# A pool of weight pieces moved to the top of the memory, and a ring of its own for each operand of the MLP's second product

## The chip, the cores and the metric

The kernel runs on one core of one Trainium2 chip. The metric is the device time of one execution in microseconds (us). Before the change the median of three runs is 2457.29 us (2456.69 to 2461.17).

## What is computed

The reference is one layer of a hybrid encoder on 1024 tokens of width 1024, all in float32:

```
shift1, scale1, gate1, shift2, scale2, gate2 = split(silu(c) @ w_ada + b_ada, 6)
h = rms_norm(x, norm1_w) * (1 + scale1) + shift1
q, k, v, xBC, z, dt, gates = split(h @ w_in)            # 1024, 256, 256, 3072, 2048, 64, 2048 columns
attn = attention(rope(rms_norm(q)), rope(rms_norm(k)), v)      # 16 heads on 4 key heads
ssd  = mamba2(silu(conv5(xBC)), z, dt)                  # forward and backward, chunks of 128
merged = sigmoid(gates[:1024]) * (attn @ w_attn_out) + sigmoid(gates[1024:]) * (ssd @ w_ssd_out)
x = x + gate1 * (merged @ w_o)
h2 = rms_norm(x, norm2_w) * (1 + scale2) + shift2
x = x + gate2 * (relu(h2 @ w_mlp1) ** 2 @ w_mlp2)       # 4096 hidden columns
```

## The kernel before, in words

**Split operands.** Each float32 operand is split into a high part, cast to fp32r by ScalarE (`A.copy`, line 173 of the profile), and the rest as a low part, subtracted by VectorE or GpSimd (line 159). A product is three matmuls per 128 rows of the contraction: high by high, high by low, low by high, most of them with 512 moving columns. A call is `matmul(out, stationary, moving)`. The profile writes a matmul as out<-moving,stationary, so `pp<-t4h,wop` moves the tile t4h past weights from wop.

**Memory.** A tile pool takes a stretch of every partition's memory; a tag in it is a ring of `bufs` slots, and tags lie in the order in which they are first asked for. Pools open from the bottom ("left") or from the top (`side="right"`), and close in the reverse order; a later pool that lies on the same stretch waits, tile by tile, for the last users. In the kernel before the 224 KB of a partition are laid out so (KB from the bottom): constants to 20, `act` (32 tiles of 2 KB for activations) 20 to 84, then by stage, left | right:

- start and projections to q, k, v, dt and z: `p0` (84 to 153), then `p1` (84 to 163), `p1m` (108 to 120) | `tw` 164 to 216 with, upward, traw (8), twh (20), twl (20), zst (4), and `scan` 216 to 224
- from line 768 on `wp`, 84 to 108: wraw, whi, wlo, two slots of 4 KB each, for pieces of weights
- convolution inputs and conv (lines 830 to 975): `st` 108 to 156 (u2, u3, u4), `p2` 156 to 210
- attention (985 to 1140): `p3k` 108 to 140 (k1, k2, v1, q1), `p3` 140 to 212 (zall, ost, nm, pf, ph at 153 to 177, pl at 177 to 201, and small ones)
- scan of the state space part, with the output products woven in (1145 to 1395): `p4` 108 to 212
- merge (1400 to 1490): `wop` 108 to 124, `p5` 124 to 158 | `mp` 160 to 224: 32 tiles of 2 KB, first g2 (32 tiles), then wo in the same slots
- w_o, norm and the MLP's first product (1495 to 1860): `wop`, `p6`, later `c1p` and `p7`, 108 to 159 | `hp` 160 to 224: tag ops, 24 tiles (T2, T3, T4, high and low, four each) at 160 to 208, and tmp at 208 to 224
- MLP's second product (1865 to 2000): `c1p` 108 to 118, `p8` 118 to 158: ac, gate2, held slots o3 (2 of 4 KB), more slots o2 (5 of 4 KB) | `hp`, whose ops slots now hold accumulators

In a ring of 2 KB tiles the first tile takes the lowest slot, the next the highest, and then downward: T2's first high tile lies at 160, the next tile at 206, and T4 lies at 162 to 176. g2 and wo take `mp` in the same way, the half-0 tiles (wo: columns 0 to 511) at 194 to 222 and the half-1 tiles at 162 to 192 downward.

**Moving operands.** In the projections to q, k, v and z (`gemm_tm`, lines 506 to 524; `first_mm`, 372 to 380) the weights move (twh, twl, twh) and the activations are stationary. In conv (`product`, 912 to 919), in `gemm_cm` (lines 195 to 216: gates, attention and state space output products) and in the MLP's first product (`product`, 1497 to 1506) weights from `wp` are stationary and activations move. In attention the scores move k1 and k2 (1036, 1038), the values move ph and pl (1090 to 1093), and 128-column transposes of pf (1053) stand between them, four at a time. In the merge g2 moves (1483 to 1485), in w_o the tiles woh and wol (1550 to 1552).

**The MLP's first product** is one level of Strassen: for each of 16 pairs of columns the products with T2, T1, T3, B22 and T4 follow each other, twelve matmuls each (T1 and B22 lie in `act`); B11 and B21 come before them in 9 pairs, in the others earlier.

**The MLP's second product** runs three rounds of seven Strassen products of four steps (84 steps, twelve matmuls of 512 columns each) and a last plain round. `prepare(n)` splits the stationary operand a and the moving operand b of step n, `LA` = 3 steps ahead (`LA0` = 2 steps are made while the first product still runs). Both take slots from one ring, a and b in turn: whi, wlo, whi, wlo, wraw, wraw, held, held, more x5. In the plain round a takes more slots; the b of its first four steps, two tiles a step, take the same first eight slots (`held`: whi, wlo, whi, wlo, wraw, wraw, held, held) and stay for both halves of the rows; its other b tiles lie in `act`.

**Order of the work.** The tile framework puts instructions in order by a plan made when the kernel is built; where `manual_schedule` names engines, their order is as written (TensorE in attention, scan and z of group 2; TensorE, VectorE, ScalarE and SyncE in the start). SyncE (SP) issues most DMAs, ScalarE some, each in its own order.

Of the kernel before, what the change touches and what calls it, by code (L numbers as in the profile page):

```python
# [91 lines left out]
def block(ctx: ExitStack, tc: tile.TileContext, ia, out, upto=99, dbg=None):  # L92
# [51 lines left out]
    s1 = cp.tile([P, 8], F32, name="s1")  # L144
    s2 = cp.tile([P, 8], F32, name="s2")
    scs = ExitStack()
    sp = scs.enter_context(tc.tile_pool(name="scan", bufs=1, side="right"))
# [69 lines left out]

    def mod_acc(pool, sl, bufs=3, mb=2):
        acc = pool.tile([P, D], F32, name="macc", tag="macc", bufs=mb)
        for k in range(KT):  # L220
            wt = pool.tile([P, D], F32, name="wada", tag="wada", bufs=bufs)
# [6 lines left out]
        return acc  # L228

# [11 lines left out]
    twp = tws.enter_context(tc.tile_pool(name="tw", bufs=1, side="right", reuse_waits="tile"))  # L241

    def tw_raw(srcs):

        raw = twp.tile([P, 2, 512], F32, name="traw", tag="traw", bufs=2)
        c0 = 0
        for src in srcs:
            w = src.shape[1]
            dma(raw[:, :, c0:c0 + w], src.rearrange("(k p) c -> p k c", p=P))
            c0 += w  # L250
        return raw

# [18 lines left out]
    with tc.tile_pool(name="p0", bufs=1) as p0, tc.tile_pool(name="ps0", bufs=1, space=PSUM) as ps0:  # L271
# [263 lines left out]

    def mod_stream(pool, psum, part):

        for sl, mi, gt in ((3, 2, None), (4, 3, None), (2, None, g_d[0]), (5, None, g_d[1]))[2 * part:2 * part + 2]:
            acc = yield from mod_acc(pool, sl, bufs=2, mb=1)
            if gt is None:  # L540
                mod_col(acc, sl, mi, psum())
            else:
                row = pool.tile([1, D], F32, name="grow", tag="wada", bufs=2)
                dma(row, b_ada[sl * D:(sl + 1) * D].unsqueeze(0))
                for hf in range(2):
                    ns = slice(hf * 512, (hf + 1) * 512)
                    ps = psum()
                    T.matmul(ps[0:1], ones[:, 0:1], acc[:, ns], start=True, stop=True)
                    tt(V, row[:, ns], ps[0:1], row[:, ns], ALU.add)
                dma(gt.unsqueeze(0), row)  # L550
            yield 1
        if part == 0:
            scale_col(s2, 3, N2)

    with tc.tile_pool(name="p1", bufs=1, reuse_waits="tile") as p1, \
# [112 lines left out]
        def dt_stream():  # L668
# [34 lines left out]
            for nm, m, h0 in (("ef", LE, 0), ("sf", GT, 0), ("cf", ones, 0), ("eb", GE, 32), ("sb", LT, 32), ("cb", ones, 32)):  # L703
                if nm in ("ef", "eb"):
# [94 lines left out]
    with tc.tile_pool(name="p1m", bufs=1, reuse_waits="tile") as p1m, tc.tile_pool(name="ps1m", bufs=1, space=PSUM) as ps1m:  # L799

        mods = mod_stream(p1m, lambda: ps1m.tile([P, 512], F32, name="psm", tag="psm", bufs=2), 1)
# [193 lines left out]
    with tc.tile_pool(name="p3k", bufs=1, reuse_waits="tile") as p3k, \  # L995
# [3 lines left out]
        def gates_stream(pool, psp, i0, i1, bufs=2, e_lo=None):  # L999
# [5 lines left out]
            yield from gemm_cm(psp, "psg", [w_cols(w_in, OFF_G + i * P) for i in range(i0, i1)], hhi, hlo, evac, bufs=bufs, e_lo=e_lo)  # L1005

        def attn_stream():

# [4 lines left out]
            def load_head(h):  # L1013
                g = h // 4
                if h % 4 == 0:
                    k1, k2, v1 = (p3k.tile(shp, F32R, name=nm, tag=nm, bufs=2)
                                  for nm, shp in (("k1", [P, S]), ("k2", [P, S]), ("v1", [P, NT, P])))
                    dma(k1.bitcast(F32), k1_d[g])
                    kv[g] = k1, k2, v1
                qs[h] = p3k.tile([P, S], F32R, name="q1", tag="q1", bufs=2)  # L1020
# [23 lines left out]
            def turn(u, hf):  # L1044
# [3 lines left out]
                if j == 0:  # L1048
                    phs[b, hf] = p3.tile([P, 4, 512], F32R, name="ph", tag="ph", bufs=3)
                    pls[b, hf] = p3.tile([P, 4, 512], F32R, name="pl", tag="pl", bufs=3)  # L1050
                pt = ps3.tile([P, 4, P], F32, name="pst", tag="pst", bufs=2)
# [624 lines left out]
    with tc.tile_pool(name="p7", bufs=1, reuse_waits="tile") as p7:  # L1676
# [91 lines left out]
        def operand(x, slot):  # L1768
            t = slot()
            split(t[:, 0], t[:, 1], x)  # L1770
            return t

        def prepare(n):
# [266 lines left out]
```

## Time and profile before

| | us |
|---|---|
| median of three runs | 2457.29 |
| profiled execution | 2455.24 |
| its span, first to last instruction | 2453.4 |
| TensorE busy (97% of the span), 11307 matmuls | 2387.5 |
| VectorE busy | 1706.5 |
| ScalarE busy | 1092.0 |
| GpSimd busy | 829.2 |

The profile lists busy time by engine, groups of instructions (line, engine, operation, tiles, count, busy time, mean of one, idle time before and who ended it), the chain of work that ended last, and a timeline. Matmuls are pipelined, and the duration of one (389 ns and more) overlaps the next; what a matmul costs is the distance from its start to the next start. PE is TensorE, PEld its weight loads, DVE is VectorE, ACT is ScalarE, POOL is GpSimd, SP is SyncE. The mean granted TensorE clock is 0.993.

### The profile page before, as it was taken

What the parts mean: (1) busy time and instruction counts of PE and PEld (TensorE: products, weight loads), DVE (VectorE), ACT (ScalarE), POOL (GpSimd) and SP (SyncE); (2) the same over time, 40 slices, a digit from 0 to 9 for tenths busy, and PEclk for the clock granted to TensorE, in tenths of its full rate; (3) what the DMA queues carried; (4) which work ended last, traced back from release to release, by engine and by line L of the source; (5) the groups of instructions that cost most, each with busy time, mean ns of one, the idle gap of its engine ahead of it and who ended that gap; (6) DMA issues with size and microseconds to landing.
All of it is one profiled execution on the core that took longest, in us unless ns stands there. A gap on an engine that the chain in (4) does not pass through costs nothing.

```text
span 2453.4 us, 32245 instructions
## 1 busy us (share of the span) xinstructions
PE 2387.5 (97%) x11307; PEld 1900.2 (77%) x11307; DVE 1706.5 (70%) x2325; ACT 1092.0 (45%) x1884; POOL 829.2 (34%) x637
## 2 busy tenths in 40 slices
PE   8999999999989999999989999999999999999999
PEld 4998877888867777777767767787787888788887
DVE  5876435777756666666577796558568887767794
ACT  5455413555566666666333343354242222364430
POOL 0221107666611111110356665534006885023200
PEclk9999999999999999999999999999999999999999
DMA  7664751333531212111667765486325554654422
GB/s 257 185 184 139 255 170 65 95 103 111 183 114 52 91 52 80 57 53 48 223 207 222 223 209 177 142 282 202 125 86 193 196 174 159 231 172 142 153 79 83
DMA packets 288596, 366.53 MB, mean 149 GB/s; under 512 B 33962, under 2 KB 168850, under 8 KB 288434
## 3 DMA queue, kind: packets, MB, share of 16 engines
q1 hardware_dynamic: 216246, 288.77, 36.9%
q10 hardware_dynamic: 72187, 75.70, 9.1%
q8 instruction: 90, 1.47, 0.2%
q14 instruction: 73, 0.59, 0.1%
HBM read 250.54 MB, written 113.84 MB: 149 GB/s over the span
## 4 chain that ended last, share of the span: by engine, by line
PE 84%; DVE 7%; DMA 3%; issue 2%; ACT 2%; POOL 0%; ACTq 0%; SPq 0%; DVEq 0%; POOLq 0%
PE pst L1053 5%; PE psg L211 4%; PE psg L213 4%; PE psg L212 4%; PE pp L1503 4%; PE pp L1505 4%; PE pp L1504 4%; PE p L1919 3%; PE p L1918 3%; PE p L1917 3%; PE psc L916 3%; PE psc L917 3%; PE psc L918 3%; PE psq L518 3%; PE psq L519 3%; PE psq L517 3%
## 5 line engine op out<-in xcount | busy, mean ns | idle before, releaser
L1040 DVE TENSOR_REDUCE nm<-pss 128x1 f32<-128x1024 f32 x128 | 156.7, 1225 | 125.2 <-PE pss L1038 122.8
L1042 ACT ACTIVATE pf<-pss,nm 128x1024 f32<-128x1024 f32 x128 | 142.8, 1116 | 98.9 <-PE pst L1053 96.3
L159 DVE TENSOR_TENSOR pl<-pst,ph 128x512 fp32r<-128x512 f32 x256 | 167.6, 683 | 27.1 <-ACT ph L173 27.0
L1053 PEld LDWEIGHTS pst<-masks,pf 128*128 128x128 f32 x1024 | 117.5, 140 | 73.3 <-issue 33.3
L517 PE MATMUL psq<-twh,hh 128*128 128x512 f32 (+1 forms) x448 | 168.3, 380 | 3.0 <-ACT twh L173 3.0
L518 PE MATMUL psq<-twl,hh 128*128 128x512 f32 (+1 forms) x448 | 169.3, 379 | 0.9 <-DVE twl L159 0.9
L173 ACT CAST ph<-pst 128x512 fp32r<-128x512 f32 x256 | 145.7, 585 | 54.9 <-PE pst L1053 38.2
L1053 PE MATMUL pst<-masks,pf 128*128 128x128 f32 x1024 | 157.3, 276 | 13.0 <-DVE pl L159 10.6
L519 PE MATMUL psq<-twh,hl 128*128 128x512 f32 (+1 forms) x448 | 168.6, 377 | 0.0
L159 POOL TENSOR_TENSOR av<-av,rz 64x512 f32<-64x512 f32 x32 | 41.9, 1310 | 348.1 <-issue 99.3
L1917 PE MATMUL p<-o,o 128*128 128x512 f32 x400 | 153.6, 390 | 3.0 <-ACT o L173 1.6
L1918 PE MATMUL p<-o,o 128*128 128x512 f32 x400 | 155.2, 389 | 0.2 <-DVE o L159 0.2
L1919 PE MATMUL p<-o,o 128*128 128x512 f32 x400 | 153.7, 389 | 0.0
L173 ACT CAST wop<-ws 128x512 fp32r<-128x512 f32 x116 | 71.8, 621 | 124.4 <-PE pp L1505 78.7
L862 DVE SCALAR_TENSOR_TENSOR tap<-pad,cwT,tap 128x1024 f32<-128x1024 f32 x96 | 123.4, 1285 | 5.2 <-ACT tap L860 3.8
L159 POOL TENSOR_TENSOR ws<-r,r 128x512 f32<-128x512 f32 x29 | 41.4, 1428 | 220.3 <-DMA r<-in_w_mlp_dram 168.9
L159 POOL TENSOR_TENSOR sl<-sl 128x512 f32<-128x512 f32 x32 | 49.4, 1546 | 179.5 <-DVE o L159 72.4
L173 ACT CAST o<-sl 128x512 fp32r<-128x512 f32 x92 | 56.9, 623 | 104.6 <-PE p L1919 88.7
L1091 PE MATMUL pv<-pl,v 128*64 128x512 f32 x256 | 102.1, 419 | 0.0
L159 DVE TENSOR_TENSOR o<-sl,o 128x512 fp32r<-128x512 f32 x92 | 72.7, 793 | 41.3 <-ACT o L173 41.3
L211 PE MATMUL psg<-hh,whi 128*128 128x512 f32 x224 | 95.7, 427 | 1.2 <-ACT ost L1002 1.2
L517 PEld LDWEIGHTS psq<-twh,hh 128*128 128x128 f32 x448 | 84.5, 189 | 15.0 <-ACT twh L173 3.4
(457 smaller groups left out, 7035.6 us busy)
## 6 DMA issues: line engine op xcount, KB each, us to landing
ar<-r SPq DMA_DIRECT2D x100, 256.0 KB
wada<-in_w_ada_dram SPq DMA_DIRECT2D x48, 512.0 KB
r<-in_w_mlp_dram SPq DMA_DIRECT2D x32, 512.0 KB
sl<-in_w_mlp_dram SPq DMA_DIRECT2D x64, 256.0 KB
r<-in_w_in_dram SPq DMA_DIRECT2D x26, 512.0 KB
r<-ro ACTq DMA_DIRECT2D x49, 256.0 KB
r<-as SPq DMA_DIRECT2D x48, 256.0 KB
xb<-cst ACTq DMA_DIRECT2D x20, 512.0 KB
```

Source lines behind the costliest of these rows:

```text
L159: e.tensor_tensor(out=o, in0=a, in1=b, op=op)
L173: (e_hi or A.copy)(hi, src)
L211: T.matmul(ps, hi[:, k], ahi[k][half], start=k == 0, stop=False)
L517: T.matmul(o, hhi[k][half][:, sl], hi[:, k % 2, :n], start=k == 0, stop=False)
L518: T.matmul(o, hhi[k][half][:, sl], lo[:, k % 2, :n], start=False, stop=False)
L519: T.matmul(o, hlo[k][half][:, sl], hi[:, k % 2, :n], start=False, stop=k == KT - 1)
L1040: V.tensor_reduce(out=nm, in_=ps, axis=AX.X, op=ALU.max, negate=True)
L1042: A.activation(pfs[u], ps, AF.Exp, bias=nm, accum_out=zall[:, u:u + 1])
L1053: T.transpose(pt[:, k], pf[:, (hf * 4 + k) * P:(hf * 4 + k + 1) * P], ident)
L1917: T.matmul(ps, a[:, 0, sl], b[0], start=start, stop=False)
L1918: T.matmul(ps, a[:, 0, sl], b[1], start=False, stop=False)
L1919: T.matmul(ps, a[:, 1, sl], b[0], start=False, stop=stop)
```

## The change

`wp` is opened before every other pool of the right side and stays there, at 200 to 224 KB. All right pools lie 24 KB lower than before (`scan` 192 to 200, `tw` 140 to 192, `mp` and `hp` 136 to 200), and so do the left pools from `st` on.

To make room in the early stages, tiles of `p0` and `p1` are taken from `wp`: six of the seven wada slots of the start; then the two tables (wlo), the held tile that has dtraw and va (wraw), macc (wraw) and the wada tiles of the first part of `mod_stream` (whi). ls takes qn's slot. `p0` is then 84 to 129, `p1` 84 to 139, `p1m` 84 to 96.

In `tw` twh and twl are asked for first, so twh lies at 140 to 160 and twl at 160 to 180. In attention k1, k2, q1 are alone in `p3k` (84 to 108), ph and pl come first in `p3` (108 to 132 and 132 to 156), and v1 moves to `p3`, after zall, at 157 to 165.

In the MLP's second product a has a ring of six slots, all in `wp`, and b a ring of seven (five more, two held), all in `p8`; the first two steps' b stay in wlo. The plain round's list of held slots is unchanged, so its six `wp` slots lie at the top now.

```diff
+    wp = ctx.enter_context(tc.tile_pool(name="wp", bufs=2, side="right", reuse_waits="tile"))
     scs = ExitStack()
     sp = scs.enter_context(tc.tile_pool(name="scan", bufs=1, side="right"))
...
+    tw0 = [twp.tile([P, 2, 512], F32R, name=nm, tag=nm, bufs=5) for nm in ("twh", "twl")]
+
+    def tw_tile(nm):
+        return tw0.pop(0) if tw0 else twp.tile([P, 2, 512], F32R, name=nm, tag=nm, bufs=5)
...
-        hi = twp.tile([P, 2, 512], F32R, name="twh", tag="twh", bufs=5)
-        lo = twp.tile([P, 2, 512], F32R, name="twl", tag="twl", bufs=5)
+        hi, lo = tw_tile("twh"), tw_tile("twl")
...
-            wt = p0.tile([P, 2, 512], F32, name="wada", tag="wada", bufs=WADA)
+            n = (hf * KT + k) % WADA
+            if n < 6:
+                wt = wp.tile([P, 2, 512], F32, name="wada", tag=("wraw", "whi", "wlo")[n % 3])
+            else:
+                wt = p0.tile([P, 2, 512], F32, name="wada", tag="wada", bufs=WADA - 6)
...
-            tb = p1.tile([P, NT, 2, HD], F32, name=f"tab{i}")
+            tb = wp.tile([P, NT, 2, HD], F32, name=f"tab{i}", tag="wlo")
...
-        dtraw = p1.tile([P, NT, 64], F32, name="dtraw")
+        held = wp.tile([P, 1024], F32, name="held", tag="wraw")
+        dtraw = held[:, 0:512].rearrange("p (t h) -> p t h", t=NT)
+        macc = wp.tile([P, D], F32, name="macc", tag="wraw")
...
-            va = p1.tile([P, 4, P], F32R, name="va", tag="va", bufs=1)
+            va = held[:, 512:1024].bitcast(F32R).rearrange("p (t d) -> p t d", t=4)
...
-                    ls = p1.tile([P, 2, 256], F32R, name="ls", tag="va", bufs=1)
+                    ls = p1.tile([P, 2, 256], F32R, name="ls", tag="qn", bufs=1)
...
-        dts, mods = dt_stream(), mod_stream(p1, lambda: ps1.tile([P, 512], F32, name="psm", tag="psd", bufs=2), 0)
+        dts, mods = dt_stream(), mod_stream(macc, lambda: wp.tile([P, D], F32, name="wada", tag="whi"),
+                                            lambda: ps1.tile([P, 512], F32, name="psm", tag="psd", bufs=2), 0)
...
-    wp = ctx.enter_context(tc.tile_pool(name="wp", bufs=2, reuse_waits="tile"))
...
+        kv0 = [p3k.tile([P, S], F32R, name=nm, tag=nm, bufs=2) for nm in ("k1", "k2", "q1")]
+        pw0 = [p3.tile([P, 4, 512], F32R, name=nm, tag=nm, bufs=3) for nm in ("ph", "pl")]
...
-                    k1, k2, v1 = (p3k.tile(shp, F32R, name=nm, tag=nm, bufs=2)
-                                  for nm, shp in (("k1", [P, S]), ("k2", [P, S]), ("v1", [P, NT, P])))
+                    k1, k2 = kq_tile("k1"), kq_tile("k2")
+                    v1 = p3.tile([P, NT, P], F32R, name="v1", tag="v1", bufs=2)
...
-            ready[n] = (operand(a_tile(n), next(op_ring)), operand(b, next(op_ring)))
+            ready[n] = (operand(a_tile(n), next(a_ring)), operand(b, next(b_ring)))
...
-        def ring():
+        def ring(first, rest):
+            yield from first
             while True:
-                yield from HOLD
-                yield from [more_slot] * 5
-
-        op_ring, held = ring(), iter(HOLD)
+                yield from rest
+
+        a_ring = ring([wp_slot("whi")] * LA0, [wp_slot(t) for t in ("wraw", "wraw", "whi", "wlo", "whi", "wlo")])
+        b_ring = ring([wp_slot("wlo")] * LA0, [more_slot] * 5 + [held_slot] * 2)
+        held = iter(HOLD)
```

kq_tile and pw_tile hand out the tiles of kv0 and pw0 first and then ask the pool, as tw_tile does. `mod_stream` and `mod_acc` now get their accumulator and a function for wada tiles; in part 1 both are in `p1m` as before. No instruction is added to or taken from any engine, and no DMA.

More of the change, by code (lines that the diff above doesn't have):

```diff
@@ L215, in gemm_cm, with mod_acc @@
                 evac(i, half, ps)
-    def mod_acc(pool, sl, bufs=3, mb=2):
-        acc = pool.tile([P, D], F32, name="macc", tag="macc", bufs=mb)
+    def mod_acc(acc, wada, sl):
         for k in range(KT):
-            wt = pool.tile([P, D], F32, name="wada", tag="wada", bufs=bufs)
+            wt = wada()
             dma(wt, w_ada[k * P:(k + 1) * P, sl * D:(sl + 1) * D])
@@ L227, in mod_acc @@
             yield 1
-        return acc
     def mod_col(acc, sl, mi, ps):
@@ L534, in z_evac, with mod_stream @@
         return evac
-    def mod_stream(pool, psum, part):
+    def mod_stream(acc, wada, psum, part):
         for sl, mi, gt in ((3, 2, None), (4, 3, None), (2, None, g_d[0]), (5, None, g_d[1]))[2 * part:2 * part + 2]:
-            acc = yield from mod_acc(pool, sl, bufs=2, mb=1)
+            yield from mod_acc(acc, wada, sl)
             if gt is None:
@@ L542, in mod_stream @@
             else:
-                row = pool.tile([1, D], F32, name="grow", tag="wada", bufs=2)
+                row = wada()[0:1]
                 dma(row, b_ada[sl * D:(sl + 1) * D].unsqueeze(0))
@@ L799, in block @@
     with tc.tile_pool(name="p1m", bufs=1, reuse_waits="tile") as p1m, tc.tile_pool(name="ps1m", bufs=1, space=PSUM) as ps1m:
-        mods = mod_stream(p1m, lambda: ps1m.tile([P, 512], F32, name="psm", tag="psm", bufs=2), 1)
+        mods = mod_stream(p1m.tile([P, D], F32, name="macc"), lambda: p1m.tile([P, D], F32, name="wada", tag="wada", bufs=2), lambda: ps1m.tile([P, 512], F32, name="psm", tag="psm", bufs=2), 1)
         def spaced():
@@ L1005, in gates_stream, with kq_tile, pw_tile @@
             yield from gemm_cm(psp, "psg", [w_cols(w_in, OFF_G + i * P) for i in range(i0, i1)], hhi, hlo, evac, bufs=bufs, e_lo=e_lo)
+        kv0 = [p3k.tile([P, S], F32R, name=nm, tag=nm, bufs=2) for nm in ("k1", "k2", "q1")]
+        pw0 = [p3.tile([P, 4, 512], F32R, name=nm, tag=nm, bufs=3) for nm in ("ph", "pl")]
+        def kq_tile(nm):
+            return kv0.pop(0) if kv0 else p3k.tile([P, S], F32R, name=nm, tag=nm, bufs=2)
+        def pw_tile(nm):
+            return pw0.pop(0) if pw0 else p3.tile([P, 4, 512], F32R, name=nm, tag=nm, bufs=3)
         def attn_stream():
@@ L1015, in load_head @@
                 if h % 4 == 0:
-                    k1, k2, v1 = (p3k.tile(shp, F32R, name=nm, tag=nm, bufs=2)
-                                  for nm, shp in (("k1", [P, S]), ("k2", [P, S]), ("v1", [P, NT, P])))
+                    k1, k2 = kq_tile("k1"), kq_tile("k2")
+                    v1 = p3.tile([P, NT, P], F32R, name="v1", tag="v1", bufs=2)
                     dma(k1.bitcast(F32), k1_d[g])
                     kv[g] = k1, k2, v1
-                qs[h] = p3k.tile([P, S], F32R, name="q1", tag="q1", bufs=2)
+                qs[h] = kq_tile("q1")
                 dma(qs[h].bitcast(F32), q1_d[h])
@@ L1048, in turn @@
                 if j == 0:
-                    phs[b, hf] = p3.tile([P, 4, 512], F32R, name="ph", tag="ph", bufs=3)
-                    pls[b, hf] = p3.tile([P, 4, 512], F32R, name="pl", tag="pl", bufs=3)
+                    phs[b, hf] = pw_tile("ph")
+                    pls[b, hf] = pw_tile("pl")
                 pt = ps3.tile([P, 4, P], F32, name="pst", tag="pst", bufs=2)
```

## The prediction

> **What bounds the kernel now.** I read the head of the page first, then the shares of the chain that ended last.
>
> ```profile
> span 2453.4 us, 32245 instructions
> ...
> PE 2387.5 (97%) x11307; PEld 1900.2 (77%) x11307; DVE 1706.5 (70%) x2325; ACT 1092.0 (45%) x1884; POOL 829.2 (34%) x637
> ...
> PE 84%; DVE 7%; DMA 3%; issue 2%; ACT 2%; POOL 0%; ACTq 0%; SPq 0%; DVEq 0%; POOLq 0%
> ```
>
> TensorE is busy for 97% of the span, and 84% of the chain is its own work. The change adds and takes away no instruction, so it can act in two ways: what a matmul costs may depend on where its operands lie, and tiles that now share memory may wait for each other. The groups of matmuls by shape say that the first is real.
>
> ```profile
> L517 PE MATMUL psq<-twh,hh 128*128 128x512 f32 x256 | 102.9, 404 | 3.0 <-ACT twh L173 3.0
> L1091 PE MATMUL pv<-pl,v 128*64 128x512 f32 x256 | 102.1, 419 | 0.0
> L1552 PE MATMUL pso<-woh,ml 128*128 128x512 f32 x128 | 50.9, 398 | 0.5 <-DVE ml L159 0.5
> L1483 PE MATMUL psg<-g2h,whi 128*128 128x512 f32 x128 | 50.6, 395 | 0.0
> L1503 PE MATMUL pp<-t4h,wop 128*128 128x512 f32 x64 | 25.2, 394 | 0.0
> L1503 PE MATMUL pp<-b22h,wop 128*128 128x512 f32 x64 | 25.0, 390 | 0.0
> L1917 PE MATMUL p<-b,o 128*128 128x512 f32 x64 | 24.9, 389 | 0.0
> L1483 PE MATMUL psg<-gh,whi 128*128 128x512 f32 x32 | 12.4, 389 | 0.0
> ```
>
> The two forms of line 1483 are the same product from the same kind of weights. With gh moving, which lies in `act` (20 to 84 KB), one takes 389 ns; with g2h, which lies in `mp` (160 KB up), 395. Line 1503 repeats it: b22h in `act` 390, t4h in `hp` 394. The b tiles of the last round go up to 158 KB and take 389. So a moving operand is dear somewhere above 158 KB and cheap below. These durations overlap; the price is the distance between starts. The timeline of one pair of the MLP's first product gives it (each line shown is the first of twelve matmuls, and the twelve end where the next line starts):
>
> ```profile
> 1935.91 0.39 PE L1503 MATMUL pp<-b22h,wop 128*128 128x512 f32 x1
> ...
> 1938.64 0.40 PE L1503 MATMUL pp<-t4h,wop 128*128 128x512 f32 x1
> ...
> 1941.43 0.40 PE L1503 MATMUL pp<-t2h,wop 128*128 128x512 f32 x1
> ...
> 1944.23 0.39 PE L1503 MATMUL pp<-t1h,wop 128*128 128x512 f32 x1
> ...
> 1946.97 0.40 PE L1503 MATMUL pp<-t3h,wop 128*128 128x512 f32 x1
> ```
>
> High: 2.79 us for T4 and 2.80 for T2, 233 ns each. Low, just behind high ones: 2.73 for B22 and 2.74 for T1, 228 ns. The end of attention shows what settles and what doesn't:
>
> ```profile
> 1181.04 0.39 PE L1091 MATMUL pv<-pl,v 128*64 128x512 f32 x1
> ...
> 1182.89 0.40 PE L211 MATMUL psg<-hh,whi 128*128 128x512 f32 x1
> ...
> 1184.97 0.39 PE L211 MATMUL psg<-hh,whi 128*128 128x512 f32 x1
> ...
> 1186.78 0.39 PE L213 MATMUL psg<-hh,wlo 128*128 128x512 f32 x1
> ```
>
> From 1181.04 eight matmuls move pl (high) and ph (partly low) in turn: 1.85 us, 231 ns each. The next nine move hh and hl from `act` and still take 2.08 us, 231 each; the eight after them 1.81 us, 226. So the full saving is 233 less 226.5, about 6.6 ns a matmul, but it comes only in an unbroken stretch of low operands: behind a high one the low ones are dear for some matmuls more, and in a mixture each costs some 231. 128-column transposes leave the same trail, here behind eight of them in conv, whose moving operands all lie low:
>
> ```profile
> 503.37 0.48 PE L918 MATMUL psc<-u4h,wop 128*128 128x512 f32 x1
> 503.68 0.39 PE L916 MATMUL psc<-u4h,wop 128*128 128x512 f32 x1
> ...
> 505.06 0.39 PE L916 MATMUL psc<-hh,wop 128*128 128x512 f32 x1
> ...
> 507.11 0.39 PE L916 MATMUL psc<-hh,wop 128*128 128x512 f32 x1
> ```
>
> The first takes 310 ns to the next start, the following six 230 each (1.38 us), the nine after them 228 (2.05 us).
>
> **What the change moves, and its price.** All right pools go down 24 KB, so the question for each is how much of it crosses to the low side. I put the border at 160 KB (b at 158 is cheap, `mp` from 160 dear), and work the addresses out from pool sizes and the order of rings.
>
> MLP's first product: `hp`'s ops slots come to lie at 136 to 184. T4 becomes low whole, of T3 three of eight tiles (the last ones), of T2 one. T4 goes from 2.79 to 2.72 us, 0.07 a pair; with T3's last low tiles B22 loses part of its trail, 0.016; T2 stays mixed and gains nothing. 16 pairs: −1.4 us.
>
> Merge: the half-1 tiles of g2 lie at 138 to 168, low for k from 3 on, which are the last 15 of 24 matmuls in each of 8 products. (Line 1483's 128 and its two sister lines make 384 matmuls, 16 products of 24, half of them of half 1.) The first few pay the trail, so 9 to 12 gain 6.6 ns, 0.06 to 0.08 us a product: −0.6. w_o moves wo tiles from the same slots, and line 1552's 128 give the same count: −0.6.
>
> Projections to q, k, v and z: twh is now low (140 to 160), twl still high (160 to 180), and a triple moves twh, twl, twh, so this is a mixture. Line 517's row counts 256 triples of 512 columns, 768 matmuls. From 233 to the mixture's 231 it is 2 ns each: −1.5. The bounds are 0 and −5.2: all twh gain the whole 6.6 (512 × 6.6 = 3.4), and as many of 400 columns gain in proportion to their columns (512 × 3.6 = 1.8).
>
> Attention: ph and pl are both low now. Two matmuls for each of line 1091's 256: 512 at 231 could gain 4.5 each, 2.2 us, but four transposes stand every few matmuls, and the conv row shows that six behind them cost 230 anyway. I take −0.2, bounds 0 and −2.2.
>
> MLP's second product: b was low and stays low for 21 products, no gain. In the plain round six of the eight held b tiles now lie at 200 KB and more: three of its eight steps, 24 matmuls each for a half of the rows, two halves, 144 × 6.6 = +1.0 us. The first two steps' b in wlo: 24 × 6.6 = +0.2.
>
> Sum: −1.4 −0.6 −0.6 −1.5 −0.2 +1.0 +0.2 = −3.1 us.
>
> **Stationary operands.** The change also puts nearly all weights of these products at 200 KB and more, where no fp32r weights of 512-column matmuls lay before: 5,000 matmuls and over. Their loads by shape:
>
> ```profile
> L1053 PEld LDWEIGHTS pst<-masks,pf 128*128 128x128 f32 x1024 | 117.5, 140 | 73.3 <-issue 33.3 <-DVE pl L159 15.6 <-ACT zr L1066 5.0
> ...
> L880 PEld LDWEIGHTS pst<-masks,cacc 128*128 128x128 f32 x160 | 18.6, 140 | 2.6
> ...
> L1503 PEld LDWEIGHTS pp<-t4h,wop 128*128 128x128 f32 x64 | 12.0, 188 | 2.7
> ...
> L1291 PEld LDWEIGHTS pso<-pbl,bcT 128*128 128x128 f32 x56 | 10.2, 188 | 4.7 <-DVE prevb L159 1.9 <-PE psg L213 0.7
> ```
>
> cacc lies at about 200 KB and loads in 140 ns, as pf does at about 150; bcT at 176 KB loads in 188 ns, as the pieces for t4h do at 108. A load starts at once behind a matmul's start and has 227 ns, so even 6.6 ns more would be hidden. I price it at 0; the bounds are 0 and the whole 6.6 on each. The Trainium skill, page "TensorE: Matmul & The Clock Gate", section "Step-by-step: what each phase is for", says that weights come by a read port of their own and are pulled ahead of running matmuls; by that rule the cost is 0 too, but no run so far shows such weights at that height.
>
> Against all of this speaks the Trainium skill, page "SBUF — State Buffer", section "Who interferes with whom": it says that TensorE never waits for another user of the memory, and no height of an operand plays a part in it. By it the gain would be 0 and the time that of before. The rows of 389 and 395 ns differ from it, so I keep the gain as the likeliest.
>
> **New waits.** Three places, with the chain at two of them:
>
> ```profile
> 290.92 5.72 DMA cn<-cst
> 296.70 4.47 DMA wada<-in_w_ada_dram
> 301.22 1.23 DVE twl L159
> 302.46 5.62 DMA traw<-in_w_in_dram
> 308.16 1.05 ACT twh L173
> ```
>
> ```profile
> 2364.16 1.81 DVE ac L159 x3
> ...
> 2366.02 0.50 PE p L1917
> ```
>
> First, at 290 to 309 us the weights of z hang on a row of transfers (constants, wada, traw), and SyncE issues them in order. The change renames who frees the memory of these wada tiles: `p1m`, still on `p1`'s stretch, now stands on other tiles of `p1`. TensorE waits 3.0 us here for twh (line 517's row). The wait can vanish, or grow by one more transfer (wada's 4.47): bounds −3.0 and +4.5. Nothing shows which, so 0.
>
> Second, head 1's v1 now lies on memory of the convolution's inputs, so its transfer on SyncE waits for the last of them, and q1 of the same head and a weight piece are queued behind it. The convolution ends near 676 and v1 is first used near 692 (I read both off the timeline). A transfer of some 5 us, as the two rows of 4.47 and 5.62 show, fits in these 16 us, so 0, bounds 0 and +4.
>
> Third, in the plain round a held b in whi or wlo has to wait for the last a of steps 82 and 83. VectorE, which makes these tiles, works without a gap before 2366, and TensorE already waits for it (the row at 2364.16): 0, bounds 0 and +2.7, the time of a step of twelve (T1's 2.74).
>
> **Sum and time.** The profiled execution of before took 2455.24 us, 1.84 more than its span, and the median is 2457.29, 2.05 above it. 2455.24 − 3.1 is 2452.1 for a profiled execution, and in terms of the median 2454.2: I say 2454. With the bounds of the mixtures and of one wait it runs from 2447 to 2459: 3.7 lower if the projections gain all, as much again if the wait at 306 goes too; 4.5 higher if a wait grows.
>
> **Rivals.**
>
> Every low matmul gains, between high ones too. A high part moves twice, a low part once. T4's twelve, T3's four and T2's two gain 18 × 6.6 ns a pair, 1.9 us in all; the merge and w_o 16 × 15 × 6.6 = 1.6; the projections their 5.2; attention up to 2.2; the plain round takes back 1.2: −7.5 to −9.7, 2449 (2447.6 to 2449.8). The 228 to 231 ns behind high operands speaks against it; for it, that mixtures are seen here only with one operand in two high, not one in three as in the projections.
>
> A new wait decides, likeliest SyncE's at 290 to 309 us: a wada transfer that waits for a tile's last user holds up traw behind it, by one transfer more than now or by two (4.47 and 5.62), and all of it is TensorE's, since the chain runs through them already: +4.5 to +10, less 3, gives 2455.7 to 2461; with the same at v1 or in the plain round up to 2465. The measurement shows it as slower only from 8 us of wait on (3.1 and the band's 4.9). For it: the chain's rows above. Against: as many of the waits there may go.
>
> Weights at the top cost what moving operands cost. The matmul would read its array's new weights 6.6 ns later: 5,268 matmuls (by my count of the lines of conv, gates, products, merge and the MLP, whose pieces come from `wp`) × 6.6 = +35, less 3: 2489. It decides if the load, not only the stream, is in the way of the next start. Against it: the 140 and 188 ns of the load rows, and the free time behind each load. For it: only that nothing of before shows it.
>
> Height plays no part: the 6 ns come from something else that T2, T3, T4 and g2 share, their age or their neighbours, say; then 2457. Against it: the b tiles of the last round, in another pool, at 389.
>
> **How the numbers follow.** A difference under 0.2% (4.9 us) is about the least that a measurement of this kernel can tell from none: 2452.4 to 2462.2 is the same. Chances: forecast 0.50, every low matmul gains 0.18, a new wait 0.15, no part 0.10, weights 0.07. Faster: 0.14 of the forecast (its lower end, where the wait at 306 goes), 0.16 of the second, 0.02 of "no part": 0.32. Slower: 0.10 of the wait, 0.07 of weights, 0.01 of "no part": 0.18. The same: the rest, 0.50. The range takes all but the weights and the outer ends: 2446 to 2463.
>
> **What the profile after would show.** Right: t4h at 390 ns in its groups and T4's twelve at 2.72 us; g2h with a mean between 389 and 395; twh and twl near 231 ns from start to start; b of the plain round at 392 or so, where it was 389; cacc, whi and wop loads at 140 and 188 as now; the busy time of TensorE 2 to 4 us less. Wrong: b22h, or hh with whi, away from 390, which would be the weights' height; twh at 390, which is the second case; or a new row among TensorE's waits, at 306, near 692 or near 2366, of 4 us or more.

## The result and the profile after

The changed kernel takes 2485.28 us (median of four runs, 2482.67 to 2485.70) beside 2458.85 before: 1.0109 times as long, 95% interval 1.0097 to 1.0122. It is slower by 1.1%, where 2454 with a range of 2446 to 2463 was forecast. The profiled execution took 2482.67 us, its span 2480.8. Head of its page and shares of its chain:

```profile
span 2480.8 us, 32159 instructions
...
PE 2406.4 (97%) x11307; PEld 1904.9 (77%) x11307; DVE 1708.5 (69%) x2325; ACT 1094.9 (44%) x1885; POOL 824.1 (33%) x637
...
PE 78%; DVE 8%; DMA 6%; ACT 3%; issue 2%; POOL 0%; SPq 0%; ACTq 0%; DVEq 0%; POOLq 0%
```

TensorE's busy time grew from 2387.5 to 2406.4 us with the same 11307 matmuls, and its share of the chain fell from 84% to 78%. (ScalarE has one instruction more than before, a table load.) So there are two losses: matmuls that cost more, and waits. Where they lie is seen by stages, from the first product of each stage to the first of the next (in us, from the starts in the two traces):

| stage | before | after | difference |
|---|---|---|---|
| start, to the first product of `gemm_tm` | 81.5 | 91.0 | +9.5 |
| q, k, v and z | 319.7 | 323.8 | +4.1 |
| conv | 273.4 | 279.5 | +6.1 |
| attention with gates | 526.0 | 527.7 | +1.7 |
| scan with output products | 395.8 | 394.0 | −1.8 |
| merge, w_o, products with B11 and B21 | 259.3 | 259.8 | +0.5 |
| MLP, first product | 273.3 | 273.8 | +0.5 |
| MLP, second product, to the end of the span | 324.4 | 331.2 | +6.8 |

The costs of matmuls stand in the groups by shape of the changed kernel (its lines are 1 to 17 further down; those for t4h, b22h, g2h, gh, b with o, twh, woh and pl answer to the ones in the prediction):

```profile
L1934 PE MATMUL p<-o,o 128*128 128x512 f32 x400 | 155.2, 395 | 3.5 <-ACT o L174 2.7 <-DVE ac L160 0.8
L524 PE MATMUL psq<-twh,hh 128*128 128x512 f32 x256 | 103.8, 408 | 2.1 <-ACT twh L174 2.1
L1106 PE MATMUL pv<-pl,v 128*64 128x512 f32 x256 | 101.8, 418 | 0.0
L1567 PE MATMUL pso<-woh,ml 128*128 128x512 f32 x128 | 50.7, 397 | 0.0
L1498 PE MATMUL psg<-g2h,whi 128*128 128x512 f32 x128 | 49.9, 390 | 0.0
L1518 PE MATMUL pp<-b22h,wop 128*128 128x512 f32 x64 | 25.2, 394 | 0.0
L1518 PE MATMUL pp<-t4h,wop 128*128 128x512 f32 x64 | 24.9, 390 | 0.0
L1518 PE MATMUL pp<-t2h,wop 128*128 128x512 f32 x64 | 25.0, 390 | 0.0
L1934 PE MATMUL p<-b,o 128*128 128x512 f32 x64 | 24.9, 389 | 0.0
L1498 PE MATMUL psg<-gh,whi 128*128 128x512 f32 x32 | 12.6, 395 | 0.0
```

The prices have changed places. b22h and gh, in `act` and never moved, went from 390 and 389 ns to 394 and 395. t4h and g2h went from 394 and 395 to 390, and so did t2h, most of which still lies above 160 KB. The products o with o of the second product, 390 before, take 395; their row in the kernel before is

```profile
L1917 PE MATMUL p<-o,o 128*128 128x512 f32 x400 | 153.6, 390 | 3.0 <-ACT o L173 1.6 <-DVE ac L159 1.4
```

In the timeline of one pair of the MLP's first product, each line again the first of twelve:

```profile
1955.90 0.40 PE L1518 MATMUL pp<-b22h,wop 128*128 128x512 f32 x1
...
1958.69 0.39 PE L1518 MATMUL pp<-t4h,wop 128*128 128x512 f32 x1
...
1961.43 0.39 PE L1518 MATMUL pp<-t2h,wop 128*128 128x512 f32 x1
...
1964.15 0.40 PE L1518 MATMUL pp<-t1h,wop 128*128 128x512 f32 x1
...
1966.94 0.39 PE L1518 MATMUL pp<-t3h,wop 128*128 128x512 f32 x1
```

B22 and T1 now take 2.79 us (2.73 and 2.74 before), T4 2.74 and T2 2.72 (2.79 and 2.80). The height of the moving operand can't do this: B22 lies where it lay. What did change is that the weights went from the pools of the left side to those of the right.

**What left and right have to do with it.** I took the address of both operands of every matmul from the kernel's allocation. The constants at the bottom take 20,832 bytes, 40 x 512 + 352, and the operands in the left pools that matter leave 352 when their address is divided by 512. The right pools hang from 229,344 = 447 x 512 + 480 and leave 480. (Attention's ph and pl are an exception: left, but behind four tiles of 32 bytes, they leave 480 before the change.) Sorted by that, with those fp32r matmuls of 512 columns alone that follow six of their kind without a gap, the mean distance from start to start is:

| stationary, moving (rest by 512) | before | after |
|---|---|---|
| 352, 352 | 227.0 ns (3260 matmuls) | 227.1 (256) |
| 352, 480 | 232.7 (1852) | 232.8 (1039) |
| 480, 352 | none | 232.6 (2858) |
| 480, 480 | none | 227.4 (932) |

So the theory for the experiments, A: a product is cheap when the addresses of its two operands leave the same rest, dear when they don't. Dear products of 512 columns number 2624 before and 5580 after. Not all count in full: of the 1344 of gates and outputs, woven in between attention's and the scan's transposes and small products, those behind which the next start follows within 260 ns take 231.3 ns in the mean before, though they agreed there, and 232.6 after. That transposes make them dear anyway is argued from the prediction's conv rows (230 ns behind transposes); it was not tried. The 512 of attention's values are taken to be of that kind too (232.5 ns before, 231.7 after). The rest of the balance is +1092 in conv, +1128 in the MLP's second product, +192 in its first, −288 in the merge: 2124 more at 5.9 ns, 12.5 us, and with the start's 9.5 that is 22 of the 26.4 us, by the count. The rivals: B, height, as the prediction had it, with weights at the top paying as well; C, the side of the memory on which each operand lies, whatever its address.

**The waits.** In the start, TensorE's waits have a new row:

```profile
PE psq L387 <- DVE hl L160: 6.5, 4, 3.0
```

It was 0.9 before. VectorE's timeline shows what stands ahead of hl there:

```profile
61.56 0.68 DVE L160 TENSOR_TENSOR hl<-xf,hh 128x512 fp32r<-128x512 f32 x1
62.16 1.28 DVE L226 SCALAR_TENSOR_TENSOR macc<-wada,sc,macc 128x1024 f32<-128x1024 f32 x1
63.36 0.80 DVE L330 TENSOR_SCALAR xf<-pst,s,modc 128x512 f32<-128x512 f32 x1
66.24 1.28 DVE L226 SCALAR_TENSOR_TENSOR macc<-wada,sc,macc 128x1024 f32<-128x1024 f32 x1 [2.08 <-DMA wada<-in_w_ada_dram]
67.44 0.68 DVE L160 TENSOR_TENSOR hl<-xf,hh 128x512 fp32r<-128x512 f32 x1
```

macc is the sum for the next modulation. Before, macc and its wada tiles lay in `p1`, on the stretch of `p0`, and the first of these operations ran at 94.5 us. Now they lie in `wp`, which the start leaves early; the plan puts eight of them (0.75 us and seven of 1.28) between the subtractions for which TensorE waits, and VectorE even stands 2.08 us for a transfer. The windows of this time (us, busy time of TensorE, its loads, VectorE, ScalarE and GpSimd, granted clock, share of DMA, GB/s):

```profile
60.00:70.00 10.00, 6.22 (x33) 5.45 (x33) 7.67 (x11) 2.69 (x5) 0.00 (x0) 0.96 0.80 256
70.00:81.00 11.00, 11.00 (x59) 10.41 (x59) 10.32 (x12) 3.87 (x5) 0.00 (x0) 0.88 0.96 302
81.00:91.00 10.00, 7.24 (x32) 6.50 (x31) 6.25 (x9) 4.56 (x6) 0.00 (x0) 0.83 0.68 211
```

(In the kernel before the granted clock is 1.00 from 60 to 70 and from 70 to 81 us, and TensorE is busy for 10.00 and 9.74 us of them.) Theory A1 is that this order costs the start's 9 us; its rival, that the early loads themselves do, which take DMA time from the projection's weights (traw).

### The profile page after: what moved, and what is told of

Its sections match the earlier page's. It is cut to its first block, busy times and chain, and to the rows that moved or that the text cites. A ratio compares the mean times of both kernels' runs of the same rounds, so it can differ in the third digit from the quotient of the medians.

```text
span 2480.8 us, 32159 instructions
## 1 busy us (share of the span) xinstructions
PE 2406.4 (97%) x11307; PEld 1904.9 (77%) x11307; DVE 1708.5 (69%) x2325; ACT 1094.9 (44%) x1885; POOL 824.1 (33%) x637
## 4 chain that ended last, share of the span: by engine, by line
PE 78%; DVE 8%; DMA 6%; ACT 3%; issue 2%; POOL 0%; SPq 0%; ACTq 0%; DVEq 0%; POOLq 0%
PE pst L1068 5%; PE p L1935 4%; PE p L1936 4%; PE p L1934 4%; PE psg L212 4%; PE psg L214 4%; PE psg L213 4%; PE pp L1520 4%; PE pp L1518 4%; PE pp L1519 4%; PE psc L922 3%; PE psc L923 3%; PE psc L924 3%; PE psq L526 2%; PE psq L525 2%
## 5 line engine op out<-in xcount | busy, mean ns | idle before, releaser
L1934 PE MATMUL p<-o,o 128*128 128x512 f32 x400 | 155.2, 395 | 3.5 <-ACT o L174 2.7
L1935 PE MATMUL p<-o,o 128*128 128x512 f32 x400 | 157.3, 394 | 0.0
L1936 PE MATMUL p<-o,o 128*128 128x512 f32 x400 | 156.6, 394 | 0.0
L174 ACT CAST o<-ar 128x512 fp32r<-128x512 f32 x100 | 61.8, 621 | 171.4 <-PE p L1936 167.6
L160 DVE TENSOR_TENSOR o<-ar,o 128x512 fp32r<-128x512 f32 x100 | 75.3, 757 | 54.7 <-ACT o L174 54.7
L525 PEld LDWEIGHTS psq<-twl,hh 128*128 128x128 f32 x448 | 84.8, 189 | 14.9 <-DVE twl L160 4.3
```

The costliest lines, as they stand in the source:

```text
L160: e.tensor_tensor(out=o, in0=a, in1=b, op=op)
L174: (e_hi or A.copy)(hi, src)
L525: T.matmul(o, hhi[k][half][:, sl], lo[:, k % 2, :n], start=False, stop=False)
L1934: T.matmul(ps, a[:, 0, sl], b[0], start=start, stop=False)
L1935: T.matmul(ps, a[:, 0, sl], b[1], start=False, stop=False)
L1936: T.matmul(ps, a[:, 1, sl], b[0], start=False, stop=stop)
```

## The experiments

The changed kernels were timed beside runs of the kernel before on the same chip. "Empty" tiles are never written or read.

**1 and 2: 128 empty bytes at the top of the memory**, in the changed kernel and in the kernel before. All right pools move 128 bytes down and leave 352 too.

```diff
+    padp = ctx.enter_context(tc.tile_pool(name="pad", bufs=1, side="right"))
+    padp.tile([P, 32], F32, name="pad")
     wp = ctx.enter_context(tc.tile_pool(name="wp", bufs=2, side="right", reuse_waits="tile"))
```

(In the kernel before, the same two lines ahead of `scan`.)

> The changed kernel with an empty tile of 128 bytes at the very top of the memory, so that wp and all right pools lie 128 bytes lower; nothing else. Theory A (distance within 512 bytes): a product of 512 columns is cheap, 226.7 ns, if the addresses of its moving and its stationary operand leave the same rest by 512, and dear, 232.6 ns, if they are 128 bytes apart; left pools (rest 352) and right pools (480) now agree (352), so all 5580 dear matmuls of the changed kernel become cheap: rows such as hh with whi in conv, b22h with wop and o with o go from 394 ns to 389 or 390, conv is 6 us shorter, the second product of the MLP 6 us, and the time falls by 22 to 27 us to about 2460. Theory B (height, as predicted, with weights at the top paying too): 128 bytes change no height, 2485 and 394 ns as before the pad. Theory C (a side of the memory, left or right, for each operand): 2485 too.

> The kernel before the change with the same 128 empty bytes at the top of its right pools; wp stays on the left. Theory A: 2624 dear matmuls of 512 columns (T2, T3, T4, g2, wo, twh, twl, and attention's ph and pl with v1) become cheap; outside attention 2112 x 5.9 ns = 12 us, in attention about 1, so 2445; t4h with wop goes from 394 to 390 ns, g2h from 395 to 389. Theories B and C: 2458, and the rows stay at 394 and 395.

Changed kernel with the pad: 2468.52 us (1.0037 times the kernel before, 1.0023 to 1.0052), 16.8 us less than without it. Kernel before with the pad: 2449.60 (0.9967, 0.9955 to 0.9979), 7.9 us less. Groups of the changed kernel with the pad:

```profile
L1936 PE MATMUL p<-o,o 128*128 128x512 f32 x400 | 153.5, 391 | 5.2 <-ACT o L176 3.1 <-DVE ac L162 2.1
...
L1520 PE MATMUL pp<-b22h,wop 128*128 128x512 f32 x64 | 24.9, 389 | 0.0
...
L1520 PE MATMUL pp<-t4h,wop 128*128 128x512 f32 x64 | 24.9, 389 | 0.0
...
L1500 PE MATMUL psg<-gh,whi 128*128 128x512 f32 x32 | 12.5, 389 | 0.0
```

and of the kernel before with it:

```profile
L519 PE MATMUL psq<-twh,hh 128*128 128x512 f32 x256 | 101.6, 399 | 2.7 <-ACT twh L175 2.7
...
L1485 PE MATMUL psg<-g2h,whi 128*128 128x512 f32 x128 | 50.0, 390 | 0.0
...
L1505 PE MATMUL pp<-t4h,wop 128*128 128x512 f32 x64 | 24.9, 389 | 0.0
```

With weights at 200 KB and more, operands at 20 KB and at 150 KB cost the same 389 ns; with weights at 84 KB, so does t4h at 162 to 176. 128 bytes do that, which change no height and no side, so B and C fall. The conv stage of the changed kernel is back at 273.7 us (279.5 without the pad). The gain of the kernel before is less than the 12 us expected. In w_o the mean from start to start fell from 234.1 to 228.3 ns, but the stage took 98.9 us (98.7): TensorE's wait at its start is 4.1 us (3.4), and the granted clock around it is 0.91 and 0.92 in two windows of 20 us (0.93 and 0.98). The changed kernel's gain, 16.8 where 22 to 27 were expected, is short too. I had counted the 1344 products of attention and scan, which take 231.3 ns with the pad and 232.6 without it (means under 260 ns, as above). But without them 4236 products at 5.9 ns are still 25 us, so some 8 us of the count do not show in the time. The granted clock of the five executions with the pad is 0.989 to 0.992, of the four without it 0.991 to 0.992; how much of the 8 us that is stays open.

**3, 4, 7 and 8: other sizes of the pad** in the changed kernel, 64, 384, 32 and 96 bytes, one execution each.

```diff
-    padp.tile([P, 32], F32, name="pad")
+    padp.tile([P, 16], F32, name="pad")
```

(and 96, 8 and 24 in the place of 16)

> The changed kernel with 64 empty bytes at the top: operands on different sides are 64 bytes apart by 512 instead of 128. If the price depends on whether the rests agree, the rows stay at 394 and the time at 2485; if it grows with the distance, they lie between, near 392, and the time near 2473. B and C: 394 and 2485.

> The changed kernel with 384 empty bytes at the top: operands on different sides are 256 bytes apart by 512. If the rest by 256 decides, all are cheap, 389 to 390 ns and 2460; if the rest by 512, the rows stay at 394 or grow, 2485 or more. B and C: 394 and 2485.

> The changed kernel with 32 empty bytes at the top: moving left operands lie 96 bytes below their weights by 256, moving right ones 96 above. Distances so far, moving less stationary by 256: 0 takes 226.8 ns, 64 229.0, 128 232.7, 192 (64 below) 233.4. If the price rises and falls smoothly, 96 above costs 231 and 160 (96 below) 233; the time 2483 to 2486.

> The changed kernel with 96 empty bytes at the top: distances 32 above and 224 (32 below). By the same rule 227 to 228 ns for 32 above and 230 to 233 for 32 below; 2470 to 2480. If a small distance is cheaper than none, below 226.8.

Times: 2480.18, 2466.78, 2493.53 and 2486.27 us. A pad gives two distances at once, left operands past right weights and right operands past left weights. The mean distance from start to start, sorted as above:

| moving less stationary address, rest by 256 | ns a product | matmuls, run |
|---|---|---|
| 0 | 226.8 | 5058, pad 128 |
| 0 (256 by 512) | 226.8 | 3901, pad 384 |
| 32 | 233.3 | 1044, pad 96 |
| 64 | 229.0 | 1039, pad 64 |
| 96 | 233.3 | 1033, pad 32 |
| 128 | 232.7 | 1852, before |
| 160 | 234.1 | 2861, pad 32 |
| 192 | 233.4 | 2868, pad 64 |
| 224 | 233.3 | 2862, pad 96 |

The rest by 256 decides: 384 bytes do as well as 128. The smooth rise that I expected is not there: 32 bytes to either side cost the full price already, and 64 above is the one distance of a middle price. No distance is cheaper than 0. The distances other than 0 and 128 were each seen in one execution, and with one arrangement of the sides.

**5: the start's order.** A copy of the silu values at the end of VectorE's work for the start, from which macc is made. It lies in 512 bytes at the top, so no rest changes.

```diff
+    scl = padp.tile([P, 128], F32, name="scl")
...
             nxt.append(tw_split(QKV_N, traws.pop(0)))
+            V.tensor_copy(scl[:, 0:8], sc)
...
-                V.tensor_scalar(out=acc, in0=wt, scalar1=sc[:, 0:1], scalar2=None, op0=ALU.mult)
+                V.tensor_scalar(out=acc, in0=wt, scalar1=scl[:, 0:1], scalar2=None, op0=ALU.mult)
...
-                V.scalar_tensor_tensor(out=acc, in0=wt, scalar=sc[:, k:k + 1], in1=acc, op0=ALU.mult, op1=ALU.add)
+                V.scalar_tensor_tensor(out=acc, in0=wt, scalar=scl[:, k:k + 1], in1=acc, op0=ALU.mult, op1=ALU.add)
```

> The changed kernel, with one tiny VectorE copy of the silu values (8 columns) behind the last subtraction of the start; the accumulation of the modulation (macc) uses the copy, so VectorE can't take its eight operations of 1.28 us in between the subtractions of the start, as it does in the changed kernel from 60 to 85 us. The copy lies in a tile of 512 bytes at the memory's top, which leaves all rests by 512 as they are. Theory A1 (VectorE's order: wada and macc no longer wait for the start's own tiles, so their work goes ahead of the start's): the first projection ends at 81 to 82 us instead of 91, TensorE's wait for hl goes from 6.5 us to 1, and the time falls by 8 to 10 us, 2476. Rival (the early loads themselves take DMA time from traw and cost the 9 us): 2483 to 2485, since they are still issued early.

2475.18 us (1.0065, 1.0048 to 1.0082), 10.1 less than the changed kernel. Wait and windows:

```profile
PE psq L389 <- DVE hl L162: 1.1, 2, 0.9
```

```profile
60.00:70.00 10.00, 9.85 (x60) 9.33 (x59) 7.64 (x12) 4.33 (x6) 0.00 (x0) 1.00 0.81 275
70.00:81.00 11.00, 9.74 (x56) 8.99 (x55) 8.45 (x14) 5.11 (x8) 0.00 (x0) 1.00 0.35 94
```

The first products of `gemm_tm` come at 81.6 us again, and the time is the one that A1 gave. But this run alone does not exclude the rival: against the expectation the copy held back most of the early loads as well (in the changed kernel SyncE issues eight wada loads between 61 and 86 us, here none before 92), and DMA's share from 70 to 81 us falls from 0.96 to 0.35. The trace of the changed kernel decides it. From 55 to 91 us no engine waits there for traw; all but 0.3 us of TensorE's waits are for hl, and VectorE, on which hl hangs, has the macc operations ahead of it and waits 3.3 us for their wada tiles. So it was VectorE's order, A1, with the waits that this order brings along.

**6: the two rings alone**, in the kernel before. `a_ring`, `b_ring` and `held` as in the change's diff take the place of `op_ring`, nothing else.

> The kernel before, with the change's two rings of the MLP's second product and nothing else of it. All of its slots stay on the left (rest 352), so no product becomes dear. If the rings themselves cost or gain nothing: 2457 to 2458, TensorE's waits in the second product 3 us in all as before. If their waits cost what is left over in the changed kernel's second product once its products are cheap (3.9 us more than in the kernel before with the pad): 2461.

2462.01 us (1.0011, 1.0002 to 1.0021). The second product takes 327.3 us (324.4 before), and TensorE's waits in it are a little longer (4.5 us in all, 3.2 before):

```profile
PE p L1919 <- ACT o L173: 2.4, 2, 1.7
PE p L1919 <- DVE ac L159: 2.1, 1, 2.1
```

So the rings cost some 3 us by themselves (2.9 in this stage), of which these waits are a little under half; the rest is not traced to a place. The same trace has 322.8 us for q, k, v and z, where nothing was edited and the kernel before has 319.7: the changed kernel's +4.1 us in that stage is hardly more than this stage varies by itself.

**9 to 12: together.** The changed kernel with the pad of 128 bytes and the late copy; the same with the one ring; and the kernel before with the pad, with and without 128 more empty bytes ahead of attention's tiles.

```diff
             tc.tile_pool(name="ps3", bufs=1, space=PSUM, reuse_waits="tile") as ps3:
+        p3.tile([P, 32], F32, name="pad3")
```

> The changed kernel with the 128 bytes of the first run (all rests agree) and the late copy of the fifth. If the two causes add up: 2468.5 less 9 to 10, 2458.5 to 2459.5, as fast as the kernel before. If the wait of the start is only covered by dear products, less than 9 comes back, 2462 or more.

> The same with the one ring of the kernel before in the MLP's second product, in the change's memory. If the rings cost here what they cost alone in the kernel before (2.8 us, 0.6 to 5), 2455 to 2458; what is then left above the kernel before with the pad (2449.6) comes from the tiles lent and moved, 5 to 8 us. If the rings cost nothing once wp lies at the top, as in the ninth run.

> The kernel before with the pad of 128 bytes on the right (second run), and 128 empty bytes in front of attention's tiles, so that ph and pl agree by 256 with v1 too (they were the last 512 dear products). If TensorE sets the pace of attention: 512 x 5.9 ns = 3.0 us less, 2446.6. If VectorE and ScalarE do (TensorE's wait of 10.6 us for pl is the largest of the kernel), 0 to 1 us less, 2449.

> The second run's kernel once more, beside the eleventh on the same chip: 2449 to 2450, ratio 0.997.

| kernel | us | ratio to before | 95% interval |
|---|---|---|---|
| changed, pad, late copy | 2455.13 | 0.9988 | 0.9979 to 0.9998 |
| the same, one ring | 2452.03 | 0.9975 | 0.9966 to 0.9984 |
| before, pad | 2450.02 | 0.9962 | 0.9950 to 0.9975 |
| before, pad, pad in attention | 2448.03 | 0.9958 | 0.9945 to 0.9970 |

The causes add up, and somewhat more: pad and copy take off 30 us of the changed kernel (16.8 and 10.1 singly), the one ring 3 more. What is left above the kernel before with the pad, 2 us where 5 to 8 were expected, lies within the intervals. So the tiles that were lent and moved cost next to nothing once the order of the start is mended. The pad in attention can't be told from none: its stage takes 525.4 us (526.0), and its 512 products, now at a distance of 0, still take 232.0 ns each, with transposes between them. All four kernels are faster than the kernel before, the last two most.

## Why the prediction was wrong

**"So a moving operand is dear somewhere above 158 KB and cheap below."** This step failed, and most of the sum with it. The rows of gh and g2h, b22h and t4h were read rightly, 389 to 390 and 394 to 395 ns for the same product, but height was only one thing that told these tiles apart. The row that set the lower edge, b with o at 389, was misread: its tiles b are those of the last four steps, which lie in `act` at 24 to 74 KB, and not the held ones up to 158 (these go by the name o). In the kernel before the stationary operands of these products and the activations in `act` lay on the left with the same rest by 512, and the moving operands that came out dear hung from the top with another. The rows used could not separate the two, and I looked at the addresses of the moving operands alone, not at those of the weights. The runs put in its place: moving less stationary address, rest by 256; 0 costs 226.8 ns, most others 233.

**"I price it at 0" for the weights.** Wrong by some 12 us by the count above, and for a reason that none of the rivals had. "Weights at the top cost what moving operands cost" came near by its number, 2489, and it named b22h away from 390 as its sign, which came. But with the same weights at the top t4h, t2h and g2h fell to 390, which it excludes, and the pad brought b22h to 389 without a change of height. The number is near by chance: 10 us of the loss are not of that kind at all. "Height plays no part" (0.10) had the right condition, something else that T2, T3, T4 and g2 share, but took that for a property of the tiles that the change leaves alone, and so gave 2457; what stood against it, b at 389, was the misread row. The row from which I took comfort, cacc's load of 140 ns at 200 KB, says nothing on the price: loads of dear and of cheap products take the same 188 ns after the change too:

```profile
L1518 PEld LDWEIGHTS pp<-t4h,wop 128*128 128x128 f32 x64 | 12.0, 188 | 2.7
L1518 PEld LDWEIGHTS pp<-b22h,wop 128*128 128x128 f32 x64 | 12.0, 188 | 2.7
```

The Trainium skill, page "TensorE: Matmul & The Clock Gate", section "Step-by-step: what each phase is for", holds that loading the next weights takes no read bandwidth from the running matmul. No run here separates loads from streams, so none shows that sentence wrong; what they show is that the two operands are not independent in their price: the conv products of the changed kernel take a median of 232 ns from start to start without the pad and 227 with it, by the distance of the two addresses alone. What is in the way there was not tried.

**The parts of the sum.** T4 came out near its price (2.74 us; 2.72 was forecast), for a wrong reason; T2, priced at no gain, fell further (2.80 to 2.72). g2 gained in both halves, 390 in the mean, not in one. w_o, priced at −0.6 like the merge, gained nothing: woh takes 397 ns (398 before), since mh and ml lie on the left and woh on the right in both kernels. twh did not gain though it moved from 164 to 140 KB: 408 ns, and its weights in `act` are 128 bytes off before and after. The plain round's held b at 200 KB, priced at +1.0 us, came out as priced: in each half three steps of 24 products take 5.60 us instead of 5.44, about 1 us in all, though again because of the distance, their a lying on the left. Each line is the first of a step; the step from 2443.27 has its b at the top, those from 2448.87 and 2454.32 on the left:

```profile
2443.27 0.40 PE L1934 MATMUL p<-o,o 128*128 128x512 f32 x1
...
2448.87 0.39 PE L1934 MATMUL p<-o,o 128*128 128x512 f32 x1
...
2454.32 0.39 PE L1934 MATMUL p<-b,o 128*128 128x512 f32 x1
...
2459.76 0.39 PE L1934 MATMUL p<-b,o 128*128 128x512 f32 x1
```

The row of b with o, in which I looked for it, could not show it and stays at 389. The second product, priced at no change but for this and +0.2, lost 6.8 us: 984 products with a at the top and b on the left and the 144 of the plain round became dear (6.7 us by the price), and the rings alone cost 2.9 us. The kept traces divide it roughly. With the rings and agreeing addresses (pads of 128 and 384 bytes, ninth run) the stage takes 327.9, 327.3 and 325.9 us, with agreeing addresses and one ring (tenth run) 323.7: of the 331.2 some 4 us belong to the addresses and some 3 to the rings. For attention's values −0.2 was of the right size: even where they agree (eleventh run) they take 232.0 ns among the transposes, which fits the reason given.

**The new waits.** None of the three places that I named shows a loss: in the stage of z TensorE's waits for twh and twl are 4.7 us (3.9 before), in the plain round its wait for ac is 0.8 (1.4), and there is no row for v1. The rival of a wait had the kind of loss, 4.5 to 10 us, and put it at 290 us. The one that came, at 60 to 90 us, I had not looked for. I asked which tile must now wait longer for its memory; here tiles wait less, and their work goes ahead of what TensorE needs. The chain through the start of the kernel before has one of VectorE's subtractions for hl on it, at 77 us, ahead of the last products of the first projection.

**The chances.** "Slower" had 0.18, of which 0.07 went to a case that ends near the measured time by another mechanism.

## What to carry to other kernels

When the cost of an instruction differs by where its operand lies, list the addresses of all of its operands and their rests by small powers of two before drawing a border, and look for a row in which the suspected quantity varies alone. In a kernel of back-to-back matmuls let the stationary and the moving operand leave the same rest by 256 bytes: one empty tile of 128 bytes gained 8 us here, and the move of a pool to the other side lost more, some 12 us by the count. And of a tile that gets its memory earlier, ask what its work will now stand ahead of.

## What the runs showed of the hardware

For products of 512 fp32r columns the time from start to start is 226.8 ns if moving and stationary address differ by a multiple of 256 bytes, 229.0 if the moving one leaves 64 more, and 232.7 to 234.1 at the other distances tried (multiples of 32). That holds for stretches of such products without a gap, stationary operands of 128 by 128. Neither the load's duration nor the height of an operand plays a part that could be seen. In the start of the changed kernel TensorE lost more than its waits: behind the wait of 2.98 us that ends at 68.2 us and the one of 2.34 that ends at 85.9, the granted clock is 0.50 for 3.4 us each (69.2 to 72.6 and 86.2 to 89.6), products of 400 columns start 0.33 us apart there instead of 0.18, and some 1.7 us more are lost each time. In the kernel before the clock is 1.00 throughout the start. That the waits bring the lower clock on is the order in which they come, not tried by itself. From the first of the two stretches:

```profile
68.18 1.02 PE L387 MATMUL psq<-twh,hl 128*128 128x400 f32 x4 [2.98 <-DVE hl L160]
...
71.10 0.54 PE L387 MATMUL psq<-twh,hh 128*128 128x400 f32 x1
71.43 0.54 PE L387 MATMUL psq<-twl,hh 128*128 128x400 f32 x1
71.77 0.54 PE L387 MATMUL psq<-twh,hh 128*128 128x400 f32 x1
```
